# Low parts of the mixer gate weights by a negating copy and an adding transfer, with refitted order numbers

## The chip, the cores and the metric

The kernel runs on one core of one Trainium2 chip. The metric is device time in microseconds (us) of one execution. Before the change it is 1059.97 us, the median of three runs from 1059.16 to 1060.96.

The engines are named as the profile names them: PE is the matrix engine (PEld its weight loads), DVE the vector engine, ACT the scalar engine, POOL the GpSimd engine, SP the engine that only issues transfers. ACT and POOL can issue transfers too.

## The reference

One layer of a hybrid encoder over 512 tokens of width 1024. The input projection makes all branches at once, and the last 2048 of its columns are the gates:

```python
h = rmsnorm(x, mix_norm[l])
p = h @ w_in[l]
rx, ry, qkv, z, ba, gates = jnp.split(p, SPLIT_IDX, axis=-1)
y_rnn = rglru_branch(rx, ry, ...) @ w_rnn_proj[l]
y_dn = deltanet_branch(qkv, z, ba, ...) @ w_dn_proj[l]
g_rnn, g_dn = jnp.split(jax.nn.sigmoid(gates), 2, axis=-1)
x = x + (g_rnn * y_rnn + g_dn * y_dn) @ w_out[l]
h = rmsnorm(x, ffn_norm[l])
gt, up = jnp.split(h @ w_gate_up[l], 2, axis=-1)
x = x + (jax.nn.silu(gt) * up) @ w_down[l]
return rmsnorm(x, final_norm)
```

Everything is float32. The gates are 16 blocks of 128 columns, eight for the recurrent branch and eight for the DeltaNet branch. A gate block needs nothing but the normalised input and its weights, so it can be computed at almost any moment before its branch is merged.

## The kernel before

**Split products.** Every large product is made of parts in a shorter float type (fp32r): a value is split into a high part `hi = round(value)` and a low part `lo = value - hi`. `mm3` (line 633) then adds three products into one PSUM bank: for each of eight row blocks `hi` times the high part and `hi` times the low part of the input (tiles `hh` and `hl`), 16 matmuls of 512 columns, and behind them eight of `lo` times the high part. So the low part of a weight tile is needed 16 matmuls later than its high part.

**Weight tiles.** `stage` (line 596) makes one 1024x128 weight tile of 512 KB: SP loads it into a buffer `wraw` (three of them), ACT copies it with rounding into `whi` (two buffers), and DVE subtracts, `wraw - whi`, into `wlo` (two buffers). `in_proj` (line 642) calls it for a block of `w_in` and then issues `mm3`; `rnn_gate` and `dn_gate` (lines 1111 and 1118) call `in_proj` with columns from `C_G` on, and ACT applies a sigmoid to the result. Because there are two `whi` and two `wlo` buffers, the copy of a tile waits until PE has read the `whi` of the tile before the last, and the low part waits for the same of `wlo`. Other weights share the buffers: `k_proj` (line 805, for `w_rnn_proj` and `w_dn_proj`) has tiles of six row blocks, 12 and 6 matmuls.

**The order of the work.** Nothing is issued as it is written. `Rec` (its call, line 384, is the line of every instruction in the profile) records each operation with its engine, an assumed duration and its dependencies. `Plan.order` (line 150) then lists them: each engine takes, of the operations that are ready, the one with the smallest key. The key is the stage's number in the table `TIMES` times 100 ns, plus an offset inside the stage (for example 12 us earlier, `AHEAD`, for the copies of a weight tile, and 40 us earlier for its load). The result is a fixed order for each engine, which the chip follows: an engine does not go past an instruction that waits.

**What runs around the gates.** The gate tiles lie between about 180 and 680 us of the execution, among the DeltaNet groups: there DVE solves small triangular systems in long runs of short instructions, POOL masks decay matrices (`AFFINE_SELECT` on tiles that SP has loaded from `gcr`) and scales keys, and ACT takes exponentials of the masked matrices (`ngc` rows), squares, and sigmoids. ACT's function tables change on the way (`ACT_TABLE_LOAD`).

Of the kernel before, what the change touches and what calls it, by code (L numbers as in the profile page):

```python
# [8 lines left out]
F32R = mybir.dt.float32r  # L9
AF = mybir.ActivationFunctionType  # L10
ALU = mybir.AluOpType
# [3 lines left out]
P = 128  # L15
# [3 lines left out]
KD = D // P  # L19
# [5 lines left out]
C_BA, C_G = 7168, 7200  # L25
# [7 lines left out]
RELEASE = 200  # L33
LOOK = 40
TIMES = [
# [15 lines left out]
]  # L51
ENGINES = ("PE", "DVE", "ACT", "POOL", "SP")
N2, N4, NW = 14, 22, 3
AHEAD = 12.0
# [335 lines left out]
def trunk(ctx: ExitStack, tc: tile.TileContext, x, mix_norm, w_in, rg_conv_w, rg_conv_b, rg_wa, rg_ba, rg_wx, rg_bx,  # L390
# [3 lines left out]
    plan = Plan(nc)  # L394
    V, A, G, T = Rec(plan, "DVE", nc.vector), Rec(plan, "ACT", nc.scalar), Rec(plan, "POOL", nc.gpsimd), Rec(plan, "PE", nc.tensor)
    Q = Rec(plan, "SP", nc.sync)
# [3 lines left out]
    wp = ctx.enter_context(tc.tile_pool(name="wp", bufs=2))  # L400
# [10 lines left out]
    def nm(s):  # L411
        uid[0] += 1
        return f"{s}{uid[0]}"

    def new(pool, shape, tag, bufs, dt=F32):
        return plan.tile(pool, shape, dt, tag, bufs, nm(tag))

    def mmb():
        return new(ps, (P, 512), "mm", 3)
# [24 lines left out]
    def spend(us=0.0):  # L444
        plan.base += us
        plan.t = plan.base
        plan.stage += 1

    def f(ap):
        return ap.bitcast(F32)  # L450
# [142 lines left out]
    win = w_in[0].rearrange("(k p) n -> p k n", p=P)  # L593
    first_tiles = []

    def stage(src, shape, view=lambda t: t, admit=()):

        now = plan.t
        raw = new(wp, shape, "wraw", NW)
        hi = new(wp, shape, "whi", 2, F32R)  # L600
        lo = new(wp, shape, "wlo", 2, F32R)
        plan.t = now - 40
        for dst, s_ in src(raw):
            Q.dma_start(dst, s_)
        plan.t = now - AHEAD
        plan.admit = admit
        A.copy(view(hi), view(raw))
        plan.admit = ()
        V.tensor_tensor(view(lo), view(raw), f(view(hi)), ALU.subtract)
        plan.t = now  # L610
        return hi, lo

    def weights(src, kk, m=P, admit=()):
        return stage(lambda raw: [(raw[:, :kk, :m], src)], (P, 8, P), lambda t: t[:, :kk, :m], admit)

# [17 lines left out]
    def mm3(po, hi, lo, xh, xl, kk, parts=1):  # L633
        n = S // parts
        for t in range(0, S, n):
            for k in range(kk):
                T.matmul(po[:, t:t + n], hi[:, k, :], xh(k)[:, t:t + n], start=k == 0, stop=False)
                T.matmul(po[:, t:t + n], hi[:, k, :], xl(k)[:, t:t + n], start=False, stop=False)
            for k in range(kk):
                T.matmul(po[:, t:t + n], lo[:, k, :], xh(k)[:, t:t + n], start=False, stop=k == kk - 1)  # L640

    def in_proj(col, po=None, admit=()):
        spend(5.2)
        hi, lo = (weights_k if len(first_tiles) < 3 else weights)(win[:, :, col:col + P], KD, P, admit)
        po = mmb() if po is None else po
        mm3(po, hi, lo, lambda k: hh[:, k, :], lambda k: hl[:, k, :], KD, 2 if len(first_tiles) < 3 else 1)
        first_tiles.append(col)
        return po
# [90 lines left out]
    def rg_front(b):  # L739
        u, us, r, i = two(), four(F32R), four(), four()  # L740
        po = in_proj(C_RX + b * P, admit=(u, us, r, i))
        graw, ghi, glo = new(wp, (P, 4, P), "graw", 1), two(F32R, (P, 4, P)), two(F32R, (P, 4, P))
        now = plan.t
        plan.t = now - (40 if b > 2 else 12)
        Q.dma_start(graw[:, 0:2, :], wa[:, b])
        Q.dma_start(graw[:, 2:4, :], wx[:, b])
        plan.t = now - AHEAD
        A.copy(ghi, graw)
        V.tensor_tensor(glo, graw, f(ghi), ALU.subtract)
        plan.t = now  # L750
        conv(po, lambda k: rg_w(k, b), rg_b(b), u)
        split(u, us)
        for q in range(4):
            d = q % 2
            pq = axb()
            T.matmul(pq, ghi[:, q, :], us[:, 0, :], start=True, stop=False)
            T.matmul(pq, ghi[:, q, :], us[:, 1, :], start=False, stop=False)
            T.matmul(pq, glo[:, q, :], us[:, 0, :], start=False, stop=True)
            act((r if q < 2 else i)[:, d, :], pq, AF.Sigmoid, bias=pcol(0, (O_BA if q < 2 else O_BX) + 12 * d + b))
        V.tensor_tensor(i, i, u.unsqueeze(1).to_broadcast([P, 2, S]), ALU.mult)  # L760
        return r, i
# [19 lines left out]
    def rg_out(b, h_, after):  # L781
        gy = two()
        po = in_proj(C_RY + b * P, po=stb(), admit=(gy,))
        act(gy, po, AF.Gelu_apprx_tanh, after)
        V.tensor_tensor(gy, h_, gy, ALU.mult)
        y = four(F32R)
        split(gy, y)
        yr[b] = y
# [16 lines left out]
    def k_proj(wv, n, k0, kts, acts):  # L805
        spend(0.65 * kts)
        po = mmb()
        hi, lo = weights(wv[:, k0:k0 + kts, n * P:(n + 1) * P], kts)
        mm3(po, hi, lo, lambda k: acts[k0 + k][:, 0, :], lambda k: acts[k0 + k][:, 1, :], kts)
        return po  # L810
# [7 lines left out]
    def dn_front(g):  # L818
# [6 lines left out]
        for h in hs_:  # L825
            kq[h] = four()
            for j, c0 in enumerate((C_K, C_Q, C_V)):
                po = in_proj(c0 + h * P, admit=(kq[h], vT[h]))
                blk = (8, 0, 16)[j] + h
                conv(po, lambda k: dn_w(k, blk), zero_t, vT[h] if j == 2 else kq[h][:, j, :])  # L830
                convs.append(len(plan.ops) - 1)
# [434 lines left out]
    def wo_part(k2, half):  # L1266
        return wo[:, 2 * k2:2 * k2 + 2, half * 512:(half + 1) * 512]

    pos = [stb(), stb(), axb(), axb()]
    for k2 in range(4):  # L1270
        hi, lo = stage(lambda raw: [(raw, wo_part(k2, 0))], (P, 2, 512))
# [42 lines left out]
    def gate_up_plain(n):  # L1314
        pos = []
        for c0 in (n * P, D_FF + n * P):
            spend(5.5)
            hi, lo = weights(wg[:, :, c0:c0 + P], KD) if n == 0 else weights_k(wg[:, :, c0:c0 + P])
            po = mmb() if c0 else stb()
            mm3(po, hi, lo, lambda k: hh2[:, k, :], lambda k: hl2[:, k, :], KD, 2)  # L1320
            pos.append(po)
        s_ = two()
        act(s_, pos[0], AF.Silu)
        for h in range(2):
            o = 256 * (h ^ n % 2)
            V.tensor_tensor(fa[n // 2][:, n % 2, o:o + 256], s_[:, h * 256:(h + 1) * 256], pos[1][:, h * 256:(h + 1) * 256], ALU.mult)
# [302 lines left out]
```

## Time and profile before

| what | value |
|---|---|
| median of 3 runs | 1059.97 us (1059.16 to 1060.96) |
| span of the profiled execution | 1059.7 us |
| PE, share of the span busy | 99% |
| DVE | 82% |
| ACT | 64% |
| POOL | 5% |
| the 16 transfer engines, mean | 116 GB/s |
| instructions | 17669 |

A group row of the profile gives engine, operation, output and input tiles by the program's names, shape, count, then the busy time in us and the mean ns of one, and behind the second bar the idle time of the engine just ahead of them and what ended it. A row of a timeline gives start and length in us. Busy time of PE is the union of its matmuls: each shows about 0.39 us, but the next starts 0.227 us after it.

### The profile page before, as it was taken

The numbers are of one execution on the slowest core, as the hardware profiler recorded it, in microseconds if no ns is written. First come the engines' busy times: TensorE is split into PE (matmuls) and PEld (weight loads), VectorE is DVE, ScalarE is ACT, GpSimd is POOL, SyncE is SP. The second block draws the span as 40 slices with busy tenths as digits, with TensorE's granted clock in tenths as the row PEclk, the third lists the DMA queues.
The fourth block names the chain that finished last, engine by engine and source line by source line (L and its number), as shares of the span: only waits on it lengthen the run. The fifth ranks groups of instructions, "written<-read, shape, count | busy, mean of one in ns | idle before, by whom it ended". The sixth has DMA issues, their size and how long they took to land.

```text
span 1059.7 us, 17669 instructions
## 1 busy us (share of the span) xinstructions
PE 1044.6 (99%) x6731; PEld 909.9 (86%) x6731; DVE 872.0 (82%) x1606; ACT 676.7 (64%) x1244; POOL 56.0 (5%) x109
## 2 busy tenths in 40 slices
PE   8999999999999999999999999999999999999997
PEld 7888887888879887988888798889999999998786
DVE  7679899769876796599489657679999988989998
ACT  7897997887454766874865535447454454545664
POOL 2000000202000230020010000000000000000000
PEclk9999999999999999999999999999999999999999
DMA  8233232233530352224203314566585342435642
GB/s 239 61 109 90 81 104 75 70 110 91 143 94 23 90 148 81 70 60 110 57 20 95 86 33 147 167 211 224 179 249 160 101 119 81 120 100 192 206 139 100
DMA packets 174389, 122.83 MB, mean 116 GB/s; under 512 B 5952, under 2 KB 160720, under 8 KB 174304
## 3 DMA queue, kind: packets, MB, share of 16 engines
q1 hardware_dynamic: 172832, 118.41, 37.4%
q10 hardware_dynamic: 1184, 3.15, 0.8%
q8 instruction: 53, 0.87, 0.4%
q0 software_dynamic: 288, 0.13, 0.1%
q14 instruction: 32, 0.26, 0.1%
HBM read 113.78 MB, written 7.90 MB: 115 GB/s over the span
## 4 chain that ended last, share of the span: by engine, by line
PE 79%; ACT 8%; DVE 7%; DMA 3%; issue 2%; POOL 0%; SPq 0%; DVEq 0%; ACTq 0%; POOLq 0%
PE mm L384 49%; PE ax L384 20%; PE st L384 11%; ACT t L384 5%; DVE t L384 4%; ACT L384 2%; DVE na L384 1%; ACT whi L384 1%; DVE wlo L384 1%; DMA wraw<-in_w_in_dram 1%; DMA wraw<-in_w_gate_up_dram 0%; ACT ax L384 0%; DMA t<-in_x_dram 0%; DMA wraw<-in_w_down_dram 0%; DMA graw<-in_rg_wx_dram 0%
## 5 line engine op out<-in xcount | busy, mean ns | idle before, releaser
L384 DVE TENSOR_TENSOR t<-t,t 128x512 fp32r<-128x512 f32 (+19 forms) x466 | 227.7, 500 | 19.1 <-ACT t L384 10.8
L384 PE MATMUL mm<-hh,whi 128*128 128x512 f32 (+2 forms) x648 | 230.0, 364 | 0.4 <-ACT hh L384 0.3
L384 PE MATMUL mm<-hl,whi 128*128 128x512 f32 (+2 forms) x648 | 229.4, 363 | 0.8 <-DVE hl L384 0.8
L384 ACT CAST whi<-wraw 128x1024 fp32r<-128x1024 f32 (+3 forms) x139 | 129.9, 936 | 129.8 <-PE mm L384 79.1
L384 DVE TENSOR_TENSOR wlo<-wraw,whi 128x1024 fp32r<-128x1024 f32 (+3 forms) x138 | 150.1, 1088 | 70.0 <-ACT whi L384 31.7
L384 PE MATMUL mm<-hh,wlo 128*128 128x512 f32 (+1 forms) x632 | 147.0, 363 | 0.0
L384 PE MATMUL ax<-t,t 32*32 32x32 f32 (+3 forms) x1062 | 140.8, 285 | 1.6 <-issue 1.1
L384 PEld LDWEIGHTS mm<-hl,whi 128*128 128x128 f32 (+1 forms) x648 | 122.0, 188 | 17.9 <-DVE hl L384 1.2
L384 PEld LDWEIGHTS mm<-hh,whi 128*128 128x128 f32 (+1 forms) x648 | 122.0, 188 | 17.8 <-ACT hh L384 0.5
L384 PEld LDWEIGHTS ax<-t,t 128*128 128x128 f32 (+1 forms) x1062 | 109.4, 159 | 19.6 <-issue 2.9
L384 PEld LDWEIGHTS mm<-hh,wlo 128*128 128x128 f32 x632 | 109.1, 189 | 17.3
L384 ACT CAST t<-t 128x512 fp32r<-128x512 f32 (+2 forms) x128 | 81.9, 652 | 49.2 <-DVE t L384 47.3
L384 PE MATMUL mm<-t,t 128*128 128x256 f32 (+1 forms) x468 | 91.3, 336 | 0.1
L384 ACT ACT_TABLE_LOAD x69 | 88.5, 1283 | 3.1 <-PEq L1615 1.7
L384 DVE SCALAR_TENSOR_TENSOR t<-mm,par,t 128x511 f32<-128x511 f32 (+1 forms) x108 | 79.3, 743 | 10.3 <-ACT t L384 9.1
L384 PE MATMUL mm<-t,whi 128*128 128x512 f32 x320 | 83.4, 396 | 0.5 <-ACT whi L384 0.5
L384 PEld LDWEIGHTS mm<-t,t 128*128 128x128 f32 x468 | 72.7, 190 | 9.3 <-DVE t L384 0.5
L384 PEld LDWEIGHTS mm<-t,whi 128*128 128x128 f32 x320 | 59.2, 188 | 13.5 <-ACT whi L384 1.1
L384 ACT ACTIVATE t<-t 128x128 f32<-128x128 f32 (+4 forms) x86 | 47.1, 558 | 27.7 <-DVE t L384 26.2
L384 ACT CAST t<-wraw 128x1024 fp32r<-128x1024 f32 (+1 forms) x51 | 44.9, 881 | 20.8 <-DMA wraw<-in_w_gate_up_dram 11.3
L384 DVE TENSOR_TENSOR t<-wraw,t 128x1024 fp32r<-128x1024 f32 (+1 forms) x51 | 51.3, 1007 | 4.3 <-ACT t L384 4.2
L384 PE MATMUL mm<-t,wlo 128*128 128x512 f32 x160 | 42.7, 393 | 0.0
(210 smaller groups left out, 1704.1 us busy)
## 6 DMA issues: line engine op xcount, KB each, us to landing
wraw<-in_w_in_dram SPq DMA_DIRECT2D x72, 512.0 KB, 3.7
wraw<-in_w_gate_up_dram SPq DMA_DIRECT2D x44, 512.0 KB, 3.8
wraw<-in_w_rnn_proj_dram SPq DMA_DIRECT2D x16, 384.0 KB, 3.5
bg<-in_w_down_dram SPq DMA_DIRECT2D x11, 512.0 KB, 4.5
sums<-bg SPq DMA_DIRECT2D x11, 512.0 KB, 4.2
wraw<-sums SPq DMA_DIRECT2D x11, 512.0 KB, 4.1
wraw<-in_w_down_dram SPq DMA_DIRECT2D x22, 256.0 KB, 2.7
wraw<-in_w_down_dram SPq DMA_DIRECT2D x11, 512.0 KB, 3.6
```

Of the source, the lines that this page charges most:

```text
L384: self.plan.add(e, lambda: real(*a, **kw), outs, ins, cost, tail, table)
```

## The change

For the 16 gate tiles a new function `weights_t` takes the place of `stage`. ACT still copies the raw tile into `whi`. ACT then writes `-whi` into `wlo` (an `ACTIVATE`, shown as `wlo<-whi`), and POOL issues a transfer that adds the raw tile onto it, from SBUF to SBUF: `wlo = -hi + raw`. DVE's subtraction of these tiles is gone. All other tiles keep `stage`. The table `TIMES` has new numbers throughout, so that all engines' orders change.

```diff
 TIMES = [
-    -187643, -118769, -184225, -128312, -118391, -104675, -104478, -23120, -15870, -23110, -75762, -33567, -65832,
...
+    -189495, -119127, -185490, -128083, -118851, -105821, -101588, -34700, -17493, -22592, -73712, -35225, -65143,
...
 ]
...
+    def weights_t(src, admit=()):
+
+        now = plan.t
+        raw = new(wp, (P, 8, P), "wraw", NW)
+        hi, lo = new(wp, (P, 8, P), "whi", 2, F32R), new(wp, (P, 8, P), "wlo", 2, F32R)
+        plan.t = now - 40
+        Q.dma_start(raw, src)
+        plan.t = now - AHEAD
+        plan.admit = admit
+        A.copy(hi, raw)
+        plan.admit = ()
+        A.mul(lo, f(hi), -1.0)
+        G.dma_start(lo, raw, accum_op=ALU.add)
+        plan.t = now
+        return hi, lo
...
     def in_proj(col, po=None, admit=()):
         spend(5.2)
-        hi, lo = (weights_k if len(first_tiles) < 3 else weights)(win[:, :, col:col + P], KD, P, admit)
+        if col >= C_G:
+            hi, lo = weights_t(win[:, :, col:col + P], admit)
+        else:
+            hi, lo = (weights_k if len(first_tiles) < 3 else weights)(win[:, :, col:col + P], KD, P, admit)
```

Three places of the orders, with the program's buffer numbers. Before, DVE around the gate tile whose low part is `wlo936_1016` (its product goes to the bank `mm937_1017`); the `t` rows are the triangular solve of a DeltaNet group:

```order
L384 TENSOR_TENSOR wlo460_540<-wraw458_538,whi459_539 128x768
L384 TENSOR_TENSOR t2611_691<-t2611_691,t2612_692 128x30
L384 TENSOR_TENSOR t2612_692<-t4610_690,t2611_691 128x29
L384 TENSOR_TENSOR t2611_691<-t2611_691,t2612_692 128x29
L384 TENSOR_TENSOR t493_173<-t493_173,mm473_553 128x512
L384 TENSOR_TENSOR t2612_692<-t4610_690,t2611_691 128x56
L384 TENSOR_TENSOR wlo936_1016<-wraw934_1014,whi935_1015 128x1024
```

With the change this low part is no longer in DVE's order. ACT's order there, from the copy of the gate tile `whi939_1019` ahead of it (`ngc` rows are the exponentials of masked decay matrices, each after POOL's `AFFINE_SELECT`; the `zero_t` row is the first step of a convolution):

```order
L384 CAST whi939_1019<-wraw938_1018 128x1024
L384 ACT_TABLE_LOAD
L384 ACTIVATE t4605_685<-t4605_685,ngc89_169 128x128 x4
L384 ACTIVATE t4606_686<-t4606_686,ngc89_169 128x128 x4
L384 ACTIVATE t4722_802<-t4722_802,ngc89_169 128x128 x4
L384 ACTIVATE t4673_753<-mm677_757,zero_t57_137,par54_134 128x512
L384 ACTIVATE wlo940_1020<-whi939_1019 128x1024
```

Between the copy and the negation of this tile stand a table load, twelve exponentials and a convolution step. The next gate tiles in the same order of ACT, and in POOL's order behind it:

```order
L384 CAST whi935_1015<-wraw934_1014 128x1024
L384 ACTIVATE wlo936_1016<-whi935_1015 128x1024
L384 CAST whi841_921<-wraw840_920 128x1024
L384 ACT_TABLE_LOAD
L384 ACTIVATE t496_176<-mm941_1021 128x512
L384 ACTIVATE wlo842_922<-whi841_921 128x1024
L384 CAST whi943_1023<-wraw942_1022 128x1024
```

```order
L384 DMA wlo940_1020<-wraw938_1018 128x1024
L384 AFFINE_SELECT t4723_803<-t4723_803 128x512
L384 AFFINE_SELECT t4726_806<-t4726_806 128x512
L384 AFFINE_SELECT t4723_803<-t4723_803 128x512
L384 AFFINE_SELECT t4726_806<-t4726_806 128x512
L384 DMA wlo936_1016<-wraw934_1014 128x1024
L384 DMA wlo842_922<-wraw840_920 128x1024
L384 AFFINE_SELECT t4727_807<-t4727_807 128x512 x2
L384 DMA wlo944_1024<-wraw942_1022 128x1024
```

Each `DMA` row waits for ACT's negation, and the `AFFINE_SELECT` rows behind it wait with it. PE's order with the change, from the last reading of the `wlo` buffer that `wlo936_1016` takes over (`wlo476_556`) to the first product of that gate tile (16 with `whi935_1015`, behind them the eight with the low part):

```order
L384 MATMUL mm473_553<-t4444_524,wlo476_556 128x512
L384 MATMUL mm457_537<-t4414_494,whi459_539 128x512
L384 MATMUL mm457_537<-t4420_500,whi459_539 128x512 x2
L384 MATMUL mm457_537<-t4432_512,whi459_539 128x512 x2
L384 MATMUL mm457_537<-t4438_518,whi459_539 128x512 x2
L384 MATMUL mm457_537<-t4444_524,whi459_539 128x512 x2
L384 MATMUL mm457_537<-t4408_488,wlo460_540 128x512
L384 MATMUL mm457_537<-t4414_494,wlo460_540 128x512
L384 MATMUL mm457_537<-t4420_500,wlo460_540 128x512
L384 MATMUL mm457_537<-t4432_512,wlo460_540 128x512
L384 MATMUL mm457_537<-t4438_518,wlo460_540 128x512
L384 MATMUL mm457_537<-t4444_524,wlo460_540 128x512
```

So 9 + 6 + 16 = 31 matmuls lie between the release of that buffer and the first use of the new low part. Behind it three gate tiles follow each other directly (`mm937`, `mm843`, `mm945`), and over the whole program six of the 16 gate tiles have exactly 40 matmuls of 512 columns there: all 24 of the tile between, and their own first 16.

28 rows, old and new, of the table TIMES are left out of this document.

## The prediction

> **What bounds the kernel now.** I read the page first, then the stretches, then who waited for whom, then the timelines of one stretch with gate tiles in it.
>
> ```profile
> PE 1044.6 (99%) x6731; PEld 909.9 (86%) x6731; DVE 872.0 (82%) x1606; ACT 676.7 (64%) x1244; POOL 56.0 (5%) x109
> ```
>
> ```profile
> 0.00:20.00 20.00, 15.63 (x94) 14.53 (x95) 13.40 (x37) 13.81 (x28) 6.81 (x21) 0.91 0.92 250
> 20.00:200.00 180.00, 179.09 (x864) 148.76 (x862) 154.17 (x194) 158.78 (x226) 0.61 (x2) 1.00 0.32 91
> 200.00:350.00 150.00, 149.84 (x936) 125.55 (x935) 113.20 (x221) 97.03 (x191) 18.06 (x28) 1.00 0.31 88
> 350.00:420.00 70.00, 68.80 (x463) 56.08 (x463) 55.96 (x122) 48.80 (x108) 14.69 (x24) 1.00 0.41 115
> 420.00:580.00 160.00, 158.70 (x1140) 135.76 (x1133) 122.15 (x303) 109.19 (x252) 15.83 (x34) 1.00 0.25 68
> ...
> 1040.00:1060.00 20.00, 12.95 (x66) 10.91 (x64) 14.89 (x35) 8.49 (x21) 0.00 (x0) 0.90 0.30 106
> ```
>
> The columns after the stretch are the busy time of PE, PEld, DVE, ACT and POOL, then PE's clock, the busy share of the transfer engines and GB/s. PE stands still for 4.4 us at the start and 7.0 us at the end, where no gate tile is. Of the 560 us from 20 to 580 it lacks 0.91 + 0.16 + 1.20 + 1.30 = 3.6 us. That is the whole room for a gain between the ends: no work of PE is removed, so relief on DVE can buy at most those 3.6 us, and whatever makes PE wait is added almost in full. ACT has the room for more work (48.8 of 70 us in the fourth stretch), so ACT's total is not the question. The question is when a low part is ready.
>
> ```profile
> DVE wlo L384 <- PE mm L384: 21.8, 14, 5.3
> ACT whi L384 <- PE mm L384: 85.1, 57, 3.9
> ```
>
> Copies and subtractions wait for PE, not for loads: two buffers each are the limit, so a low part can't be begun earlier than PE releases its buffer.
>
> **The change part by part.** What goes and comes, each by its row:
>
> ```profile
> L384 DVE TENSOR_TENSOR wlo<-wraw,whi 128x1024 fp32r<-128x1024 f32 x95 | 115.9, 1221 | 55.6 <-ACT whi L384 21.5 <-PE mm L384 19.0 <-ACT t L384 13.5
> L384 ACT CAST whi<-wraw 128x1024 fp32r<-128x1024 f32 x95 | 99.6, 1050 | 94.8 <-PE mm L384 60.1 <-issue 13.8 <-PE ax L384 13.4
> L384 ACT ACTIVATE t<-t 128x1024 f32<-128x1024 f32 x22 | 22.9, 1055 | 0.2
> L384 ACT ACT_TABLE_LOAD x69 | 88.5, 1283 | 3.1 <-PEq L1615 1.7 <-DVE so L384 0.2
> ```
>
> DVE loses 16 x 1.22 = 19.5 us. ACT gains 16 activations of 128x1024, 16 x 1.06 = 17 us; its order also has 75 table loads in place of 69, 6 x 1.28 = 7.7 us. Both fit under PE's work, so I cost their totals at nothing; if that cover were gone, the 25 us of ACT would show. POOL gains 16 issues:
>
> ```profile
> 6.23 0.70 POOL L384 DMA_DIRECT2D dtb<-in_dn_dt_bias_dram  x1
> ```
>
> At 0.7 us each they are 11 us on an engine with 5% of use, but in its fixed order: behind a waiting issue stand masks, and behind these ACT's exponentials.
>
> The cost that matters is the time from the issue of the adding transfer to its landing; call it T. No row shows one. The nearest:
>
> ```profile
> t<-in_dn_norm_dram POOLq DMA_DIRECT2D x1, 0.5 KB, 4.5
> t<-in_dn_conv_w_dram POOLq DMA_DIRECT2D x1, 48.0 KB, 4.9
> dtb<-in_dn_dt_bias_dram POOLq DMA_DIRECT2D x1, 8.0 KB, 6.5
> gcr<-t SPq DMA_DIRECT2D x1, 32.0 KB, 1.5
> wraw<-in_w_in_dram SPq DMA_DIRECT2D x72, 512.0 KB, 3.7
> ```
>
> POOL's transfers need 4.5 us with next to no bytes; SP's show what bytes cost, 3.7 - 1.5 = 2.2 us for 480 KB more. Lower bound: the 4.5 us came from a burst of nine issues while x was loading (the transfer engines were 92% busy in the first 20 us), so an isolated one might need only SP's 1.5 plus POOL's 0.7 for the issue, and 2.2 for the bytes: 4.4 us. Upper bound: 4.5 us and the bytes twice, since an adding transfer reads its target as well: 4.5 + 4.4 = 8.9 us. I take 4.5 + 2.2 + 0.5 = 7.2 us, near the plain sum of POOL's own row and the only row of that size, with a little for the second read.
>
> [...]
>
> Now the time that the order leaves for T. One stretch of the trace shows gate tiles directly behind each other:
>
> ```profile
> 390.02 1.52 PE L384 MATMUL mm<-t,wlo 128*128 128x512 f32 x6
> 395.01 1.98 PE L384 MATMUL mm<-hh,wlo 128*128 128x512 f32 x8
> 400.45 1.98 PE L384 MATMUL mm<-hh,wlo 128*128 128x512 f32 x8
> ```
>
> ```profile
> 390.22 1.05 ACT L384 CAST whi<-wraw 128x1024 fp32r<-128x1024 f32 x1 [3.11 <-PE mm L384]
> 397.57 1.28 ACT L384 ACTIVATE t<-t,ngc 128x128 f32<-128x128 f32 x4
> ```
>
> ```profile
> 392.43 1.22 DVE L384 TENSOR_TENSOR wlo<-wraw,whi 128x1024 fp32r<-128x1024 f32 x1
> ```
>
> PE's pace is 24 matmuls in 400.45 - 395.01 = 5.44 us, 0.227 us each. The buffer of the second gate tile was released at 390.02 + 1.52 = 391.54; its low part was used at 400.45, that is 8.9 us later (40 matmuls by the pace: 9.1). The subtraction was over at 393.65, with 6.8 us to spare. With the change those 9.1 us must hold a handoff, the negation of 1.06, another handoff, and T: with 0.2 us for each handoff (my estimate; the copy at 390.22 began within 0.1 us of the release of its buffer) 7.6 us are left for T. So the six gate tiles with 40 matmuls in their window are hidden up to T = 7.6 us, by 0.4 us in my case. Several others have more.
>
> Tighter ones, by the changed order. The tile of `wlo936` has 31 matmuls: 31 x 0.227 = 7.0, less 1.06 and 0.4, leaves 5.6 us; it costs 7.2 - 5.6 = 1.6. The tile of `wlo940` is late because of ACT. From the release of its `whi` buffer to its first low product stand 50 matmuls of 512 columns and four short ones, 50 x 0.227 = 11.4 and some 1.5 us, 12.9 in all. On ACT the copy (1.05), a table load (1.28), twelve exponentials (three times the 1.28 for four), a convolution step (0.78) and the negation (1.06) make 8.0 us:
>
> ```profile
> L384 ACT ACTIVATE t<-mm,zero_t,par 128x512 f32<-128x512 f32 x24 | 18.6, 778 | 16.4 <-PE mm L384 16.2
> ```
>
> 12.9 - 8.0 - 0.4 leaves 4.5 us for T and a wait of 2.7. The first gate tile of that stretch (`wlo717`) has eight squares with their sums and a copy between its own copy and its negation, and the last one of all (`wlo920`) has its copy late on ACT; I put both together at 1.5 us, by the same kind of reckoning. The tiles behind `wlo936` have 40 matmuls and the time that PE has just lost, so they cost nothing. Sum: 1.6 + 2.7 + 1.5 = 5.8 us.
>
> The refitted numbers also move everything else. I take that at nothing: the 3.6 us that PE lacks now may go or come back elsewhere, so plus or minus 2 us is its size. The profiled execution is 1059.7 us, the median 1059.97, so the one stands for the other. Forecast: 1060.0 + 5.8, about **1066 us**. A PE that waits gives ACT and POOL time to get ahead for the next tile, so this sum does not grow with the number of tiles as long as T stays under 7.6.
>
> **The rivals.**
>
> *Hidden.* T is near its lower bound, 4.4 to 5.3 us. Then only `wlo940` could wait, for under 1 us, and the time is 1058 to 1062, no change. For it: isolated issues, transfer engines busy a quarter to two fifths of the time in these stretches. [...] Against it: every POOL row is at 4.5 or more with almost no bytes.
>
> *Late everywhere.* T is at 8.5 us or more, because reading the target doubles the bytes or is slow. Then the six tiles with a budget of 7.6 pay too: at 8.9, 6 x 1.3 = 7.8 us, and the four tight ones 3.3 + 4.4 + 2 x 2.5 = 12.7, together 20 us: 1080. With ten tiles waiting, each further half microsecond of T adds 5 us, so 1075 to 1095. For it: the second read. [...]
>
> *Faster.* The waits of PE came from DVE's long run of small solves, and a DVE with 19.5 us less to do ends them. The trace has such waits:
>
> ```profile
> PE ax L384 <- DVE t L384: 2.0, 3, 1.2
> ```
>
> It can give at most the 3.6 us that PE lacks, so 1056 to 1057.8; it decides if T is also hidden. DVE's runs hold a gate's subtraction only here and there, so this is little likely.
>
> **How the numbers follow.** The forecast, 1062.2 to 1074, has a chance of 0.53; late everywhere 0.22; hidden 0.15; faster 0.10. A difference under 0.2% (2.1 us) cannot be told from none here. Slower by over 0.2% is then 0.53 + 0.22 = 0.75, no change 0.15, faster 0.10. The range reaches from the middle of the hidden case, 1058.5, to T somewhat over its upper bound, 1086; the forecast's own range is 1062 to 1074.
>
> **What would show it.** The POOL rows `wlo<-wraw` among the transfers give T directly: 6.5 to 8 us for my case, under 5.3 for hidden, over 8.5 for late everywhere. Waits of PE (or PEld) on the transfer into `wlo` should appear, some 4 to 8 us in a few waits, the largest of them on the tiles of `wlo940` and `wlo936` between 350 and 420 us, where PE's busy share falls most. The group of DVE's 128x1024 subtractions should fall from 95 to 79, with a new group of 16 activations `wlo<-whi` of about 1.06 us. I am wrong if PE waits for these tiles while T is under 5 us (then ACT's or POOL's order is late, not the transfer), if the time is lost after 700 us, where no gate tile is, or if it is gained there.

## The result and the profile after

The changed kernel takes 1065.31 us (median; 1063.98 to 1067.28), the kernel before 1061.27 us (median of six, 1059.16 to 1063.27): a ratio of 1.0045, with a 95% interval from 1.003 to 1.0059. It is slower by 4 to 5 us. A repetition, shown further down, gives 1.0044.

From the page of the changed kernel, the row of the engines and the row of the new transfers:

```profile
PE 1045.0 (98%) x6731; PEld 908.3 (85%) x6731; DVE 852.9 (80%) x1590; ACT 701.6 (66%) x1266; POOL 67.8 (6%) x125
...
wlo<-wraw POOLq DMA_DIRECT2D x16, 512.0 KB, 4.7
```

DVE has 19.1 us less to do, ACT 24.9 us more, POOL 11.8 us more, and PE's work is the same. The last column of the last row is the median from issue to landing, 4.7 us.

The stretches, with the columns as they stand in the prediction:

```profile
200.00:350.00 150.00, 148.40 (x930) 123.71 (x929) 113.03 (x222) 97.04 (x182) 16.54 (x26) 1.00 0.32 87
350.00:420.00 70.00, 67.90 (x362) 55.15 (x364) 50.63 (x117) 50.50 (x103) 17.60 (x31) 1.00 0.61 147
420.00:580.00 160.00, 158.41 (x1236) 133.86 (x1223) 107.49 (x269) 120.08 (x270) 21.39 (x40) 1.00 0.35 84
580.00:700.00 120.00, 119.58 (x798) 99.28 (x797) 77.96 (x175) 60.25 (x106) 3.48 (x4) 1.00 0.47 130
700.00:1000.00 300.00, 300.00 (x2221) 287.07 (x2220) 280.07 (x486) 160.50 (x283) 0.00 (x0) 1.00 0.51 161
```

PE lacks 1.60 us from 200 to 350 us (0.16 before), 2.10 from 350 to 420 (1.20 before), 1.59 from 420 to 580 (1.30 before), 0.42 after that, and nothing from 700 to 1000 us. The waits of PE say for whom, in total, times and longest:

```profile
PE mm L384 <- DMA wlo<-wraw: 1.8, 1, 1.8
PE ax L384 <- DVE na L384: 1.2, 1, 1.2
PE ax L384 <- ACT t L384: 1.0, 2, 0.7
PE mm L384 <- ACT t L384: 0.9, 2, 0.4
```

One single wait is for the new transfer. The other larger one, 1.2 us for DVE's `na`, comes at 251 us, in the making of DeltaNet's matrices, where no gate tile is.

The waits that the profile lists between 20 and 1040 us sum to 5.7 us, and to 3.4 before. These 2.3 us are about half of the 4 to 5 that were timed. Busy time hides the rest, because a matmul is shown with 0.39 us where the next starts after 0.227: a gap of up to 0.16 us leaves no hole. I therefore took from the trace the time between the starts of two matmuls, less the median for the same shape in the kernel before, and summed it from 20 us on. By that measure PE loses 19.8 us before and 24.2 us after, 4.4 more, which is the timed difference. (The two levels depend on how finely shapes are told apart: 16.0 and 20.4 with the tiles' names as well. The difference is the same.) By stretch, after less before: 1.8 from 200 to 350, 0.4 from 350 to 420, 3.1 from 420 to 580, 1.1 from 580 to 700, minus 1.8 behind 700, and minus 0.2 ahead of 200.

The two places of the prediction, in PE's timeline of the changed kernel:

```profile
389.03 1.98 PE L384 MATMUL mm<-hh,wlo 128*128 128x512 f32 x8
...
403.41 2.12 PE L384 MATMUL mm<-hh,wlo 128*128 128x512 f32 x8 [1.79 <-DMA wlo<-wraw]
...
419.51 0.75 PE L384 MATMUL ax<-t,na 32*32 32x32 f32 x64
```

and in POOL's:

```profile
383.96 0.90 POOL L384 DMA_DIRECT2D wlo<-wraw  x1 [1.15 <-PE ax L384]
...
396.01 0.90 POOL L384 DMA_DIRECT2D wlo<-wraw  x1 [4.60 <-DVE t L384]
```

The first is the tile of `wlo940`: issued at 383.96, landed 4.6 us later by the trace, at 388.5, and used at 389.03 without a wait. The second is the tile of `wlo936`: issued at 396.01, landed only at 403.4, 7.4 us later, and PE waited 1.79 us for it. Around that issue SP's queue had this:

```profile
388.60 5.61 SPq L384 DMA_DIRECT2D wraw<-in_w_in_dram  x3
394.27 0.88 SPq L384 DMA_DIRECT2D t<-gcr  x1
```

and the transfers' view of the stretch from 395 to 404 us shows, by queue, packets, MB and share of the 16 engines:

```profile
q1 hardware_dynamic: 2338, 1.17, 48.7%
q0 software_dynamic: 215, 0.82, 46.1%
q8 instruction: 1, 0.02, 0.6%
```

The first of the three weight loads had landed at 392.5 us. The other two and the broadcast from `gcr` were under way, and together with POOL's transfers they kept the transfer engines busy 95% of that stretch. The packets and the semaphore's updates in the trace split the lateness in two. The transfer's first packet came 2.48 us after the issue, where isolated ones have it after 1.45, while the packets of the loads and the broadcast ran until 399 us. With that, 15 of the 16 transfer engines had reported by 401.80 us, 5.8 us after the issue. The sixteenth reported only at 403.37. Between the two stands the one packet of the `instruction` queue, 16 KB, from 401.29 us for 0.89 us, and the last small packet of the transfer comes behind it. PE was ready at 401.62. So without this one packet its wait would have been some 0.2 us, and about 1.6 of the 1.79 us belong to it. That it held that engine is inferred from the times, as the trace does not name the engine of a packet. Another tile shows the same without any load beside it: issued at 506.86 us, it had 15 engines done after 4.54 us and the sixteenth after 6.24, with one such packet under way.

```profile
q8 instruction: 1, 0.02, 1.3%
...
wlo<-wraw POOLq DMA_DIRECT2D x1, 512.0 KB, 6.2
```

These are rows of the transfers' view from 506 to 514 us. PE did not wait for that tile. By these times the low part of `wlo936` was late, 7.4 us where undisturbed ones take 4.5, because it shared the transfer engines, with loads and with the instruction queue, not because it is always slow.

### The profile page after: what moved, and what is told of

Same layout as the page of the kernel before. It is cut to its first block, busy times and chain, and to the rows that moved or that the text cites. A ratio compares the mean times of both kernels' runs of the same rounds, so it can differ in the third digit from the quotient of the medians.

```text
span 1062.8 us, 17740 instructions
## 1 busy us (share of the span) xinstructions
PE 1045.0 (98%) x6731; PEld 908.3 (85%) x6731; DVE 852.9 (80%) x1590; ACT 701.6 (66%) x1266; POOL 67.8 (6%) x125
## 4 chain that ended last, share of the span: by engine, by line
PE 79%; ACT 8%; DVE 7%; DMA 2%; issue 2%; ACTq 0%; POOL 0%; SPq 0%; DVEq 0%; POOLq 0%
PE mm L384 45%; PE ax L384 22%; PE st L384 12%; ACT t L384 5%; DVE t L384 5%; ACT L384 2%; DVE wlo L384 1%; DVE na L384 1%; ACT whi L384 1%; DMA wraw<-in_w_in_dram 1%; DMA wlo<-wraw 1%; DMA t<-in_x_dram 0%; DMA graw<-in_rg_wx_dram 0%; ACTq L384 0%; ACT na L384 0%
## 5 line engine op out<-in xcount | busy, mean ns | idle before, releaser
L384 DVE TENSOR_TENSOR t<-t,t 128x512 fp32r<-128x512 f32 (+23 forms) x466 | 228.3, 505 | 26.8 <-ACT t L384 18.4
L384 DVE TENSOR_TENSOR wlo<-wraw,whi 128x1024 fp32r<-128x1024 f32 (+3 forms) x122 | 130.9, 1074 | 64.7 <-ACT whi L384 34.9
L384 PEld LDWEIGHTS mm<-hh,wlo 128*128 128x128 f32 x632 | 109.1, 189 | 19.5 <-DMA wlo<-wraw 2.2
```

Source lines behind the costliest of these rows:

```text
L384: self.plan.add(e, lambda: real(*a, **kw), outs, ins, cost, tail, table)
```

## The experiments

Two theories were left. **Landing**: the loss is the transfer's way from issue to landing, T. **Order**: the loss is in the refitted table and in moving work to engines whose order is fixed. The runs swap how the low part is finished in the new order, move the new operations into the old order, and then size T itself. All ratios are to the kernel before on the same chip.

### The new order, with DVE adding

```diff
+        plan.ops[-1] = plan.ops[-1][:1] + (lambda: nc.vector.tensor_tensor(lo, f(lo), raw, ALU.add),) + plan.ops[-1][2:]
```

Behind `G.dma_start` in `weights_t`: DVE adds the raw tile at the place where POOL issued the transfer.

> The changed kernel's order of every engine, with the copies and the 16 negations on ACT kept; DVE adds the raw tile to the negated one at the place where POOL issued the transfer, so only the transfers and their landing are gone (DVE has 16 x 1.22 us back). Theory 'landing' (the loss comes from the transfers: PE waited 1.8 us for one, and the rest follows from their traffic and their issues on POOL): ratio to before 0.999 to 1.001. Theory 'order' (the one wait of 1.8 us is all that the transfers cost; the other 2 to 3 us come from the refitted order): 1.002 to 1.004, no wait of PE for a transfer, PE still lacking about 1.6 us between 200 and 350 us.

Measured: 1074.98 us, 1.0154 (1.014 to 1.0168). Both theories missed. PE's waits and two stretches of this kernel (stretch rows as above):

```profile
PE ax L384 <- DVE t L384: 5.7, 3, 3.4
```

```profile
420.00:428.00 8.00, 5.99 (x137) 4.69 (x138) 1.92 (x3) 5.07 (x14) 0.00 (x0) 0.57 0.24 68
522.00:528.00 6.00, 4.99 (x137) 3.85 (x138) 1.50 (x3) 5.84 (x14) 0.00 (x0) 0.72 0.18 52
```

The largest of these three waits, 3.40 us, is at 422 us, for the end of the solve of the third DeltaNet group. Three of the additions stand in it (at 397.27, 403.52 and 410.27 us), 3 x 1.22 us, and its last transpose begins 2.8 us later than in the changed kernel. DVE's timeline, the first of the additions and that transpose:

```profile
397.27 1.22 DVE L626 TENSOR_TENSOR wlo<-wlo,wraw 128x1024 fp32r<-128x1024 f32 x1
...
421.24 0.71 DVE L384 STREAM_TRANSPOSE t<-t 128x512 f32<-128x512 f32 x1
```

And in the changed kernel:

```profile
418.47 0.71 DVE L384 STREAM_TRANSPOSE t<-t 128x512 f32<-128x512 f32 x1
```

And then something that I had not reckoned with: at the long wait the granted clock falls to 0.50 for some microseconds, which shows as 0.57 and 0.72 in the stretches above. From the clock between 20 and 1040 us I get 5.1 us lost to it in this run (the time times one less the clock, summed), and none in the kernel before or after. So the new order is slower with DVE's adding by 10 us (spans of 1073.3 and 1062.8 us): it leans on the relief that the transfers bring.

### The old order, with negation and transfer

```diff
+        def negate_and_add():
+            nc.scalar.mul(lo, f(hi), -1.0)
+            nc.gpsimd.dma_start(lo, raw, accum_op=ALU.add)
...
+        plan.ops[-1] = plan.ops[-1][:1] + (negate_and_add,) + plan.ops[-1][2:]
```

The recorded subtraction of the 16 gate tiles is replaced by the two operations at its place; the table is the one before.

> The order of before on every engine; at the place of each gate tile's subtraction ACT negates and POOL issues the adding transfer, without refitted numbers. In the trace of before five of the 16 subtractions began so shortly before their first product that 1.06 + 0.25 + 4.55 us don't fit: by 3.3, 1.7, 1.7, 1.0 and 0.1 us, 7.7 together. Theory 'landing': PE waits there, 1.003 to 1.007. Theory 'order': PE waits there too, but nothing else is lost, and the relief of DVE by 19.5 us gives up to 2 us back: 1.001 to 1.005. A rival, that the relief of DVE is worth more than the waits: below 0.998.

Measured: 1083.25 us, 1.0234 (1.022 to 1.0248). T was short here too (median 4.6 us). PE's waits:

```profile
PE mm L384 <- DMA wlo<-wraw: 6.8, 4, 3.7
PE ax L384 <- ACT t L384: 4.4, 5, 1.4
PE mm L384 <- DVE t L384: 3.3, 1, 3.3
```

These and the smaller ones behind them make most of the 21.5 us by which the span grew (1081.2 against 1059.7 us), and 3.4 us are again the clock at two of the waits. Only 6.8 us are waits of PE itself for the transfer. To see what the rest is, I left the transfer out of the tiles that have little time for it.

### The old order, with the transfer only where there is time

```diff
+        if lo.tensor.name.split("_")[0] in ('wlo591', 'wlo717', 'wlo940', 'wlo944', 'wlo842', 'wlo847', 'wlo932', 'wlo928', 'wlo948', 'wlo596', 'wlo712'):
+            plan.ops[-1] = plan.ops[-1][:1] + (negate_and_add,) + plan.ops[-1][2:]
```

The 11 tiles whose subtraction began at least 7.4 us ahead of its first product in the kernel before; the other five keep DVE's.

> The order of before; negation and adding transfer for the 11 gate tiles whose subtraction began 7.4 us or more before its first product, DVE's subtraction for the other five. If the loss of 2.3% with all 16 came from leads shorter than the landing: 0.999 to 1.001. If it came from ACT, which now waits for the low part's buffer and holds up what stands behind it in its order: over 1.004, with PE waiting for ACT and for copies rather than for transfers.

Measured: 1073.32 us, 1.0123 (1.0109 to 1.0136). PE's own waits for the transfer are gone, but 13.1 of the 24.3 us of loss (by the medians) stay. PE's longest wait:

```profile
393.08 5.46 PE L384 MATMUL mm<-t,whi 128*128 128x512 f32 x12 [3.33 <-DVE t L384]
```

It stands in the run with all 16 too, and in both the trace leads back from it to a landing. The transfer reads the raw tile, so the raw tile's buffer, one of three, is free only when the transfer has landed. SP's next load into such a buffer waits for that, and what stands behind it in SP's order waits with it. With the 11 tiles, from the transfer's issue on:

```profile
370.52 0.90 POOL L625 DMA_DIRECT2D wlo<-wraw  x1 [2.70 <-ACT wlo L624]
...
376.68 0.37 SPq L384 DMA_DIRECT2D wraw<-in_w_rnn_proj_dram  x1
377.10 1.09 SPq L384 DMA_DIRECT2D t<-gcr  x2
...
381.47 1.81 POOL L384 TENSOR_SCALAR_AFFINE_SELECT t<-t 128x512 f32<-128x512 f32 x3 [7.03 <-DMA t<-gcr]
...
382.14 2.46 ACT L384 ACTIVATE t<-t,ngc 128x128 f32<-128x128 f32 x8 [6.38 <-POOL t L384]
```

The transfer landed at 376.63 us, and the weight load, which SP had held for 13.7 us, went out 0.05 us later. In the kernel before, the same load went out at 367.93 and the broadcasts behind it from 370.26 on:

```profile
367.93 0.37 SPq L384 DMA_DIRECT2D wraw<-in_w_rnn_proj_dram  x1
370.26 1.44 SPq L384 DMA_DIRECT2D t<-gcr  x2
```

The masks wait for the broadcasts, the exponentials for the masks, DVE for the masks too (6.14 us), and PE for DVE. The wait of 3.33 us and the clock of 0.50 from 392.4 to 399.2 us (3.4 us) are 6.7 of the 12.4 us by which the span grew (1072.1 against 1059.7). The pattern comes twice: at 124 us a load held back by such a landing delays a `graw` load behind it, ACT waits 1.50 us for that, and at 137 us PE waits 1.44 us for ACT. So the landing counts in the old order although PE never waits for it.

The rest is in part ACT's fixed order, in which the negations now stand ahead of other work. In the run with all 16 the profile shows a buffer's wait that DVE had before and ACT has now:

```profile
ACT wlo L624 <- PE mm L384: 4.9, 4, 2.7
```

With the 11 tiles it is 1.6 us in two waits. How much of the loss hangs on it is not shown.

### One transfer alone

```diff
+        if lo.tensor.name.split("_")[0] in ('wlo944',):
+            plan.ops[-1] = plan.ops[-1][:1] + (negate_and_add,) + plan.ops[-1][2:]
```

The old order, and only the gate tile whose subtraction stood at 392.4 us within the solve that PE waited for at 414 us (1.20 us).

> The order of before with negation and transfer for one gate tile only (the subtraction at 392.4 us, inside DVE's solve of the third DeltaNet group, 8.0 us ahead of its product). If PE's wait of 1.2 us at 414 us is for that solve, it goes to under 0.3 us and the time is 0.05 to 0.15% under before. If ACT's extra 1.06 us there delays the next copy, no gain or 1.001.

Measured: 1059.22 us against 1060.19, 0.9992 (0.9983 to 1.0001). PE's timeline, and the stretch:

```profile
413.24 0.75 PE L384 MATMUL ax<-t,na 32*32 32x32 f32 x64
```

```profile
350.00:420.00 70.00, 69.94 (x469) 57.20 (x468) 55.20 (x121) 50.54 (x112) 15.56 (x27) 1.00 0.47 123
```

The wait is gone, and PE lacks 0.06 us in this stretch where it lacked 1.20. The whole kernel gains about 1 us, which the interval does not quite tell from nothing. It has the lowest median of this study.

### The new numbers alone

```diff
-        if col >= C_G:
+        if False:
```

The new table, with `stage` and DVE's subtraction for all tiles. The planner makes its own order out of the table for these operations, so this is a third order and not the one of the change. (The opposite, an order that the planner makes from the old table with the transfers, was not run.)

> The new table of numbers with DVE's subtraction for all tiles as before the change; the planner makes its own order from it. Theory 'landing': 0.999 to 1.001. Theory 'order': 1.002 to 1.005, with waits of PE at places that have nothing to do with gate tiles.

Measured: 1067.67 us, 1.008 (1.0067 to 1.0094). The waits are spread out; the stretch from 700 to 1000 us, where the gates are done, loses most:

```profile
700.00:1000.00 300.00, 296.30 (x2194) 283.92 (x2193) 274.64 (x475) 159.09 (x277) 0.00 (x0) 0.99 0.49 155
```

A table that was fitted to one set of operations may be worth less for another; the whole time does not say what the new table costs with the operations that it was fitted to. One stretch does:

```profile
200.00:350.00 150.00, 148.31 (x928) 123.09 (x927) 113.26 (x222) 97.95 (x184) 17.11 (x26) 1.00 0.31 87
```

PE lacks 1.69 us here without any transfer, and 1.60 in the changed kernel. DVE's rows from 239 to 250 us, ahead of the wait for `na`, have the same order in both kernels, and the wait is 1.15 us here. So this loss is the new table's.

### The one late tile by DVE

```diff
+        if lo.tensor.name.startswith("wlo936"):
+            plan.ops[-1] = plan.ops[-1][:1] + (lambda: nc.vector.tensor_tensor(lo, f(lo), raw, ALU.add),) + plan.ops[-1][2:]
```

In the changed kernel, only the tile that PE waited for is finished by DVE.

> The changed kernel and its order, but the one tile for which PE waited (issue at 396.0 us, landing 7.4 us later) gets its low part by a DVE addition at the place of the issue; the other 15 keep the transfer. If the single wait costs its own 1.8 to 2.0 us and no more: 0.2% less than the changed kernel, 1.002 to 1.0035 to before. If it also sets off what is lost later: 1.000 to 1.001. If PE has slack behind it and makes it good: 1.004 to 1.005 as the change.

Measured: 1065.22 us, 1.0066 (1.0053 to 1.0079), so nothing is gained. The wait for the transfer is gone, and another stands 16 us later:

```profile
419.69 0.75 PE L384 MATMUL ax<-t,na 32*32 32x32 f32 x64 [2.08 <-DVE t L384]
```

The changed kernel had no wait at this instruction (419.51 above). But this run does not say that the landing costs nothing, because the addition puts 1.22 us of DVE into the very solve that PE now waits for: its last transpose begins at 418.93 us, against 418.47 in the changed kernel. The kernel with the plain copy, below, has a shorter landing and no addition, and there PE reaches the same instruction 1.7 us earlier than in the changed kernel, without a wait:

```profile
417.81 0.75 PE L384 MATMUL ax<-t,na 32*32 32x32 f32 x64
```

So the wait for the landing does go away with the landing, where DVE is not loaded in its place.

### How the landing depends on adding, and on other transfers

Plain copy, which leaves out the addition, in one run and then in five:

```diff
+        plan.ops[-1] = plan.ops[-1][:1] + (lambda: nc.gpsimd.dma_start(lo, raw),) + plan.ops[-1][2:]
```

> The changed kernel with a plain copying transfer in place of the adding one (the low part is then the raw tile, so the gates' values are not the reference's); same issue, same bytes written. It prices the reading of the target. If reading the target doubles the cost of bytes: median landing about 3.2 us in place of 4.7, 0.17 us for a row of 4096 bytes in place of 0.34. If the addition is free: 4.5 to 4.7 us, and the same time.

> The changed kernel with the plain copying transfer (landing about 3.0 us in place of 4.6; the gates' low parts are then the raw tiles, so the values differ). If the landing is behind the loss: 0.3 to 0.45% under the changed kernel, within 0.1% of before. If the refitted order is: 0.1 to 0.2% under it, 1.002 to 1.004 to before.

Beside the five, the changed kernel once more:

> The changed kernel itself, timed beside the three others on one chip: 1.003 to 1.006 as before.

Measured: the one run 1063.27 us. In the five 1063.54 us with the plain copy, 1.0036 (1.0023 to 1.005), and 1064.89 us for the changed kernel, 1.0044 (1.0031 to 1.0056). The transfer's row and PE's wait with the plain copy:

```profile
wlo<-wraw POOLq DMA_DIRECT2D x16, 512.0 KB, 3.0
```

```profile
PE mm L384 <- DMA wlo<-wraw: 0.5, 1, 0.5
```

T falls from 4.8 to 3.0 us, PE's waits for the transfers from 1.6 to 0.5 us (the 0.5 is for another tile than `wlo936`), and the kernel wins 1.35 us by the medians, not clear of the intervals. About 0.1% of the 0.44% hangs on the landing; the larger part stays when the landing is short.

The packets of the two tell what T is made of. Each is 128 packets of 4096 bytes, eight rows for each of the 16 transfer engines. Undisturbed, an adding transfer has its first packet 1.45 us after the issue, then eight rows of 0.34 us, and 0.35 us to the semaphore: 4.5 us. The plain copy has 1.10 us and eight rows of 0.173 us. Adding doubled the time of a row here.

A load beside each transfer:

```diff
+        beside = new(dr, (P, 8, P), "beside", 16)
...
+            nc.sync.dma_start(beside, src)
+            nc.gpsimd.dma_start(lo, raw, accum_op=ALU.add)
```

SP sends the 512 KB of the tile once more, from DRAM to DRAM.

> The changed kernel with one more 512 KB transfer (the tile's own weights, DRAM to DRAM) issued by SP beside each of the 16 adding ones. If the landing at 7.4 us came from other transfers in flight: the quiet ones, 4.5 to 4.6 us, rise to 6 to 8 us, and PE's waits for them to 8 us or more in total. If it came from something else (POOL's issue, DVE): they stay at 4.5 to 5.5 us.

Measured in one run: 1065.36 us. The median of T rose only to 5.0 us, because SP, in its own order, often sent the extra load at another time than POOL its transfer. In the stretch around 400 us, where the loads did meet, the three transfers took 8.3, 7.6 and 6.9 us (issue to landing in the trace), and PE waited longer for the first:

```profile
PE mm L384 <- DMA wlo<-wraw: 2.8, 1, 2.8
```

So with more traffic the late landing came later, 8.3 us for 7.4, and by 1 us for PE. Here all the engines were late: 15 of the 16 had reported after 8.1 us, where it was 5.8 in the changed kernel. That shows that loads delayed this landing; it does not say that loads made the last 1.6 us of the 7.4. Since most of the loads missed, it does not size what one load costs.

### POOL doing the arithmetic itself

In the new order, POOL adds the raw tile; in the old order, POOL does the whole subtraction:

```diff
+        plan.ops[-1] = plan.ops[-1][:1] + (lambda: nc.gpsimd.tensor_tensor(lo, f(lo), raw, ALU.add),) + plan.ops[-1][2:]
```

```diff
+        plan.ops[-1] = plan.ops[-1][:1] + (lambda: nc.gpsimd.tensor_tensor(lo, raw, f(hi), ALU.subtract),) + plan.ops[-1][2:]
```

> The changed kernel and its order on every engine, but at the place of each of the 16 issues POOL adds the raw tile to the negated one by itself (an instruction of POOL, no transfer): nothing lands late, and DVE keeps its relief. Theory 'landing wait counts': PE's wait of 1.8 us goes and with it 0.1 to 0.2%: 1.002 to 1.0035, if POOL's addition takes under 4 us. Theory 'the solve behind it decides' (DVE's solve of the third DeltaNet group ends at about 419 us whatever PE waits for at 403 us, and PE stands there instead): 1.004 to 1.006, with a new wait of PE of about 1.5 us for the solve at 419 us. If POOL's addition slows DVE or is longer than 5 us: over 1.006.

> The order of before on every engine, with POOL in place of DVE for the 16 gate subtractions (raw minus high part, no negation, no transfer): the relief of DVE by 19.5 us without ACT's extra work and without a landing. If DVE's relief is worth something, 0.997 to 0.999, and PE's wait for the solve at 414 us goes from 1.2 to under 0.5 us. If POOL needs over 3 us for one, or stands in its order waiting for a buffer with masks behind it: 1.003 and more, with waits of ACT and DVE for POOL.

Measured: 1083.14 us in the new order, 1.0223 (1.0208 to 1.0238), and 1065.66 us in the old one, 1.0061 (1.0047 to 1.0075). The low part was ready sooner than with the transfer (2.4 us in place of 4.7), and the kernel was much slower in the new order. DVE shows why. One piece of the solve, ten small instructions, in the changed kernel:

```profile
395.45 2.72 DVE L384 TENSOR_TENSOR t<-t,t 128x54 f32<-128x54 f32 x10
```

and with POOL's additions in the new order, DVE and POOL:

```profile
396.02 4.81 DVE L384 TENSOR_TENSOR t<-t,t 128x54 f32<-128x54 f32 x10
```

```profile
396.36 2.40 POOL L626 TENSOR_TENSOR wlo<-wlo,wraw 128x1024 fp32r<-128x1024 f32 x1 [4.38 <-ACT wlo L384]
```

The same ten instructions take 2.09 us longer: the growth is most of POOL's 2.40 us. Three additions of POOL fall into this solve, one DVE instruction grows at each, by 2.1, 2.2 and 2.1 us, and at the end of the solve PE waits:

```profile
424.78 1.08 PE L384 MATMUL ax<-t,na 32*32 32x32 f32 x64 [6.77 <-DVE t L384]
```

The rows show the growth, not what makes it. In the new order the transfer is the better form (1.0045 against 1.0223). In the old order POOL's own subtraction is (1.0061 against 1.0234): it needs neither the negation on ACT nor a landing.

## Why the prediction was right, and where it was not

**Direction and size** came as forecast, 4 to 5 us for 5.8. But the terms of the sum did not all come as written.

**The totals** were costed rightly at nothing. DVE lost 19.1 us (19.5 reckoned), ACT gained 24.9 (24.7), POOL 11.8 (11). The subtractions of 128x1024 fell from 95 to 79, and a group of 16 negations with a median of 1.06 us stands in ACT, beside 75 table loads. Within DVE's order the relief is real: where one subtraction alone was moved, PE's wait of 1.20 us was gone.

**T failed.** I took 7.2 us; the median is 4.7 and the quiet value 4.5, at my lower bound. The step that failed took the 4.5 us of POOL's rows at the start of the kernel for a fixed cost. The fixed part is 1.45 + 0.35 = 1.8 us, and the rest, 2.7 us, is bytes. The argument for the lower bound, that those rows were slow because of the burst at the start, is what the packets show: in the kernel before, the first of the nine has its first packet 3.5 us after the issue, the isolated adding transfers after 1.45. The upper bound was right to count the bytes' part twice for an adding transfer: a row that is added took 0.34 us and one that is copied 0.173, and the plain copy's T was 3.0 us.

**`wlo936`** was priced at 1.6 us and cost 1.79 (1.6 in the repetition), at the place that was named. The reason was another: a T of 7.4 us that came from two loads and a broadcast in the same microseconds (some 1.2 us) and from one engine that reported 1.6 us after the others, not a T that is always so long. The budget of 5.6 us was right. That T passed it by the forecast amount at just this tile was luck: with T = 4.6 the tile would have been hidden.

**`wlo940`** was priced at 2.7 us and cost nothing; ACT's late negation was to leave 4.5 us for T; by the trace it left 5.1 (383.96 to 389.03), and T was 4.6. **`wlo717` and `wlo920`**, 1.5 us together, did not appear as waits for the transfer either. By the prediction's own signs the landing was the hidden rival's, under 5.3 us, while the time was that of the forecast.

**The refit** was taken at nothing, within 2 us, and this is the mis-sized term: some 3 us are left for it. The runs bound it. A shorter landing gives back 1.35 us, and with it the kernel is still 0.36% slower than before, 3.4 us by the medians. So of the 4 to 5 us about a quarter goes with the shorter landing, and the rest belongs to the new order with the work moved in it. Two pieces of it can be named. The wait of 1.2 us for DVE's `na` at 251 us was 0.2 before, and it stands in every run with the new table, with plain copies (1.0 us), with DVE's additions (1.2) and with no negation and no transfer at all (1.15): it is the table's. The waits of 1.0 and 0.9 us for ACT's `t` were 0.2 us in all before. What makes the many gaps under 0.3 us between 420 and 580 us is **open**: they are there in both traces of the changed kernel (8.6 and 8.4 us beyond the pace, against 5.5 before), so they belong to the order, but part of them may be only another mix of matmuls in that stretch. No run has the new operations in an order made from the old table, and so the order's part is what remains, not a measured difference. The right total is thus partly luck: the landings were priced at 5.8 us, PE waited 1.79 us for one of them, and a term put at nothing made up for the rest.

**The faster rival** had its mechanism right and its balance wrong. A DVE with less to do does end a wait, but that is shown for one tile of 16 alone. In the old order the others brought waits of PE, of ACT and of SP's loads with them.

**Nothing was lost after 700 us**, as forecast, and PE did wait for a transfer with T under 5 us in the median, but the one that it waited for took 7.4.

**One reader was left out.** The prediction asks when PE needs the low part. It has no term for the raw tile's buffer, which the transfer holds until it lands. In the changed order SP's queue waits for these landings too (132 us in 16 waits), but no wait of PE was traced to it there; in the old order it made half of the loss that is left with 11 tiles.

## What to carry to other kernels

In a kernel whose engines follow a fixed order, relief for an engine is worth only the waits that the bounding engine has on it: find these, and try first the one instruction that stands in front of each. Price a moved step by every in-order queue that it joins, for a step that waits for a buffer hands that wait to all that stands behind it (behind one held load POOL's masks stood for 7.03 us and ACT's exponentials for 6.38). Ask also which buffer a transfer reads: here the next load into it, and all behind that load in its queue, waited for the landing, one load for 13.7 us in all. Take a transfer's fixed cost from a quiet place of the trace or from its packets (1.8 us here), not from the burst at the start (4.5), and look in the other queues for what will share the transfer engines at the moment of its issue: the landing of 7.4 us was as late as the last of the 16, and 15 had reported after 5.8.

## What the runs showed of the hardware that I had not expected

**Some waits cost more than their length.** In the runs with long waits of PE the granted clock fell to 0.50 for 3.4 or 6.8 us at them (rows above, 0.57 as a mean over 8 us). Summed, 5.1 us were lost so with DVE's additions, 6.8 us with POOL's in the new order, 3.4 us with all transfers in the old order and as much with the 11, 1.7 us with the new numbers alone. Between 20 and 1040 us none was lost in the kernel before, after, or in the other runs. The length of the wait alone does not decide it in these runs. The clock fell at a wait of 2.12 us in the run with the new numbers alone,

```profile
732.56 0.56 PE L384 MATMUL mm<-hh,t 128*128 128x256 f32 x1 [2.12 <-ACT t L384]
```

```profile
732.00:736.00 4.00, 3.44 (x16) 3.44 (x17) 2.01 (x3) 2.49 (x7) 0.00 (x0) 0.58 0.89 296
```

while one of 2.9 us in the old order with POOL's subtractions and one of 2.8 us with the load beside did not.

**An adding transfer took twice a copying one's time per row**, 0.34 against 0.173 us for 4096 bytes, and its issue held POOL longer, 0.89 against 0.54 us:

```profile
L384 POOL DMA_DIRECT2D wlo<-wraw x16: 862/887/907, 185.1 to 687.5; - x16
```

```profile
L626 POOL DMA_DIRECT2D wlo<-wraw x16: 527/539/587, 184.6 to 684.8; - x16
```

The first row is the changed kernel's, the second that of the plain copy; the three numbers are the least, the median and the largest in ns.

**A DVE instruction grew at each of POOL's additions.** An addition of 128x1024 took POOL 2.40 us where it took DVE 1.22, and in the solve above 2.1 to 2.2 us were added to the DVE instruction that met it.

**A landing was as late as its last transfer engine.** Of the transfer issued at 506.86 us, 15 engines had reported after 4.54 us and the last after 6.24, with a 16 KB packet of the instruction queue under way (row above) and no load.
